# Matmuls on neighbouring strips of the TensorE array, queued as one group behind the member whose input comes last

## Chip, core and metric

The kernel runs on one core of one Trainium2 chip. The metric is device time in microseconds (us), the median of three timed runs. Besides these there is one profiled execution, whose records are what the views of the profile show.

## What is computed

Two layers of a diffusion backbone over 512 latent and 256 context tokens of width 1024, in float32. Layer 0 mixes tokens with neighbourhood attention (8 heads of 64) beside a chunked mLSTM; layer 1 with latent attention. Each layer then has a gated feed-forward part with hidden width 2816. In front of and behind each part stands an RMS norm:

```python
def rms_norm(x, g):
    xf = x.astype(jnp.float32)
    y = xf * lax.rsqrt(jnp.mean(xf * xf, axis=-1, keepdims=True) + EPS)
    return (y * g.astype(jnp.float32)).astype(x.dtype)
```

The change touches two things: the sums of squares under these norms, and in `neighbourhood_attention` the two products of the weights with the values, over the window and over the context keys:

```python
        return (jnp.einsum('bhqk,bkhd->bqhd', p[..., :nl], v_band)
                + jnp.einsum('bhqk,bkhd->bqhd', p[..., nl:], v_c))
```

## The kernel before

Activations lie feature-major: eight tiles of 128 features (index k or m) by 512 latent (`SX`, or its halves `SH`) and 256 context columns (`SC`). Each large product takes weights and activations split into a high and a low part, three matmuls for each piece of 128 features: `mm` (L139) is the helper that issues nearly all of them, so they all carry L139 and are told apart by their output tile: `yps` (output projections), `pu`/`puf` (feed-forward up), `pd`/`pdl` (feed-forward down; `pdl` is the last group), `qps`/`kvp` (the first projections of layer 1), `qp`/`sp` (queries and scores of the neighbourhood attention).

**Sums of squares.** A norm needs, for each token, a sum over 1024 features. The engines square the eight feature tiles one after another; `sums4` (L387) takes four squares at a time and issues four matmuls (L390) against a 128x32 matrix of ones. Each goes to its own strip of 32 columns of the array, and so to its own 32 partitions of one PSUM tile: `ysum` for the norm behind a part (`YNorm.put`, squares `ysq` made by ScalarE), `pss` for the norm ahead of the next part (`YNorm.chain` and `RawNorm.chain`, squares written over `acc`). Two calls make one sum. Then a chain runs over several engines (`sums_bc`, L393): ScalarE copies the sums (`srow`), TensorE adds the four strips (`psc`), VectorE and GpSimd form the inverse root (`rv`, `ry`), and TensorE spreads it over all partitions (`bcy` or `bcm`). `sums4` is called 30 times.

**Neighbourhood attention.** `na_attn` handles two heads at once. Head 0 uses array columns and output partitions 0 to 63, head 1 the other 64. For each block of 128 keys the transposed weights `pT` come from ScalarE for head 0 and from VectorE for head 1, and `products` (L879) issues matmuls into `ops`, the two heads in turn; L948 does the same for the context queries into `opc` from `ptc` (shown as `pTc`).

**What sets the order.** Each engine runs its instructions in one fixed order, made at build time by a scheduler of the framework from the program, the dependencies and its own estimate of when each input will be there. Matmuls of one call may therefore end up apart, with matmuls of other tiles between them.

Of the kernel before, what the change touches and what calls it, by code (L numbers as in the profile page):

```python
# [18 lines left out]
TX = 512  # L19
TC = 256  # L20
# [44 lines left out]
def hybrid_backbone_kernel(ctx: ExitStack, tc: tile.TileContext, *aps):  # L65
    nc = tc.nc
    V, S, G, PE = nc.vector, nc.scalar, nc.gpsimd, nc.tensor
    a = dict(zip(_DEV, aps))
    out = aps[len(_DEV)]
# [34 lines left out]
    def ps_x(name):  # L104
        return ps_t("x", name)
# [29 lines left out]
    V.memset(mhalf, -0.5)  # L135


    def mm(o, l, r, start, stop):
        PE.matmul(out=o, lhsT=l, rhs=r, start=start, stop=stop)  # L139

    def tr(o, i):
        PE.transpose(out=o, in_=i, identity=ident[0:i.shape[0], 0:i.shape[0]])  # L142
# [1 line left out]
    def act(o, i, func=AF.Copy, **kw):  # L144
        S.activation(out=o, in_=i, func=func, **kw)  # L145
# [35 lines left out]
    def proj(o, w, x, cols, ks=tuple(range(KD)), first=True, last=True):  # L181

        whi, wlo = w
        xhi, xlo = x
        for lo, hi, oo in cols:
            for k in ks:
                wh = whi[:, k * 128:(k + 1) * 128]
                wl = wlo[:, k * 128:(k + 1) * 128]
                oa = o[:, oo:oo + hi - lo]
                mm(oa, wh, xhi[:, k, lo:hi], first and k == ks[0], False)  # L190
                mm(oa, wh, xlo[:, k, lo:hi], False, False)
                mm(oa, wl, xhi[:, k, lo:hi], False, last and k == ks[-1])
# [38 lines left out]
    ones32 = const.tile([128, 32], F32, name="ones32")  # L231
# [154 lines left out]

    def sums4(ps, w, srcs, first, last):  # L387

        for i, src in enumerate(srcs):
            PE.matmul(out=ps[32 * i:32 * i + 32, 0:w], lhsT=ones32, rhs=src, start=first, stop=last,  # L390
                      tile_position=(0, 32 * i))

    def sums_bc(ps, sg, name):  # L393

# [7 lines left out]
    class YNorm:  # L402
# [10 lines left out]
        def put(self, m, src):  # L413
            w = self.sg.w
            if self.wide:
                if m == 0:
                    act(self.acc, src, AF.Square)
                else:
                    sq = scratch("ysq")
                    act(sq[:, :w], src, AF.Square)  # L420
                    tt(G, self.acc, self.acc, sq[:, :w], ALU.add)
                return
            if m % 2 == 0:
                self.t = sqp.tile([128, 512], F32, tag="sq", name="ysq")
            sq = self.t[:, 256 * (m % 2):256 * (m % 2) + w]
            act(sq, src, AF.Square)
            self.sq.append(sq)
            if m % 4 == 3:
                sums4(self.ps, w, self.sq[-4:], m == 3, m == KD - 1)

        def chain(self, x, y, Gt, mod=None, done=None):
# [13 lines left out]
            for k in range(KD):  # L445
                stt(y(k), y(k), Gt[:, k, c:c + 1], bc[:, :w], ALU.mult, ALU.mult)
                tt(G if k in (RVF if done and mod else RVO) else V, x(k), y(k), x(k), ALU.add)
                if mod:
                    act(y(k), x(k), AF.Square)
                    if k % 4 == 3:  # L450
                        sums4(ps2, w, [y(k - 3 + i) for i in range(4)], k == 3, k == KD - 1)
                else:
                    done(k)
                yield
# [17 lines left out]
    class RawNorm(YNorm):  # L472


        def chain(self, x, y, Gt, mod, done):
            sg = self.sg
            w, c = sg.w, sg.mc
            A, h = mod
            bc = sums_bc(self.ps, sg, "y")
            yield  # L480
            self.ps2 = ps_c("pss")
            for k in range(KD):
                stt(y(k), y(k), Gt[:, k, c:c + 1], bc[:, :w], ALU.mult, ALU.mult)
                tt(G if k in RVF else V, x(k), y(k), x(k), ALU.add)
                hi, lo = (t[:, k, sg.ho:sg.ho + w] for t in h)
                act(hi, x(k), AF.Copy, scale=A[:, k, c:c + 1])
                stt(lo, x(k), A[:, k, c:c + 1], fr(hi), ALU.mult, ALU.subtract)
                act(y(k), x(k), AF.Square)
                if k % 4 == 3:
                    sums4(self.ps2, w, [y(k - 3 + i) for i in range(4)], k == 3, k == KD - 1)  # L490
                yield
# [12 lines left out]
    with ExitStack() as l0:  # L504
# [20 lines left out]
        for k in range(KD):  # L525
            sq = x0p.tile([128, T], F32, tag="sq0", name="sq0", bufs=4)
            act(sq, x0[:, k, :], AF.Square)
            for lo, hi in ((0, TX), (TX, T)):
                PE.matmul(out=pss[32 * (k % 4):32 * (k % 4) + 32, lo:hi], lhsT=ones32, rhs=sq[:, lo:hi], start=k < 4,
                          stop=k >= 4, tile_position=(0, 32 * (k % 4)))  # L530
# [73 lines left out]
        for k in range(KD):  # L604
            for gp, lo, hi in ((gpx, 0, TX), (gpy, TX, T)):
                PE.matmul(out=gp[32 * (k % 4):32 * (k % 4) + 32, 0:hi - lo], lhsT=wg[:, k, :], rhs=x0[:, k, lo:hi],
                          start=k < 4, stop=k >= 4, tile_position=(0, 32 * (k % 4)))
# [87 lines left out]
        for i in range(7):  # L695
            src, dst = runs[i % 2], runs[1 - i % 2]
            for d in range(2):
                r = slice(32 * d, 32 * d + 32)
                o = 64 + (2 * d - 1) * 2 ** i
# [127 lines left out]
        def na_attn(p_, nw, bias_t, fill, qs, kd, kl, vtok):  # L827
            ops_ = ps_x("ops")
            nf = NF if p_ < 3 else NF3
            rows = ((0, 64), (64, 128))  # L830
# [32 lines left out]
            def turned(ks, Ps):  # L863

                pts = []
                for s, P in enumerate(Ps):
                    pt = ps_w("ptp")
                    for j in range(4):
                        tr(pt[:, j * 128:(j + 1) * 128], P[j][:, ks * 128:(ks + 1) * 128])
                    fill(nf[1])  # L870
                    pT = nw.tile([128, 512], F32, tag="pT", name="pT", bufs=4)
                    if s:
                        V.tensor_copy(out=pT, in_=pt)
                    else:
                        act(pT, pt)
                    pts.append(pT)
                return pts

            def products(ks, pts):  # L879

                if ks >= 2:
                    for s, (r0, r1) in enumerate(rows):
                        mm(ops_[r0:r1, 0:TX], vtok[:, 7 + ks - 2, r0:r1], pts[s], ks == 2, False)
                    return
                for j in range(4):
                    vi = VTILE[KSTART[j] + 16 * ks]
                    for s, (r0, r1) in enumerate(rows):
                        mm(ops_[r0:r1, j * 128:(j + 1) * 128], vtok[:, vi, r0:r1],
                           pts[s][:, j * 128:(j + 1) * 128], False, ks == 1 and j == 3)

            def scores_c(s):
                r0, r1 = rows[s]
# [20 lines left out]
            def turned_c(s, Pc):  # L913
                pt = ps_w("ptc")
                for kt in range(2):
                    for j in range(2):
                        tr(pt[:, (2 * kt + j) * 128:(2 * kt + j + 1) * 128],
                           Pc[:, j * 256 + kt * 128:j * 256 + (kt + 1) * 128])
                fill(nf[3])
                pT = nw.tile([128, 512], F32, tag="pT", name="pTc", bufs=4)  # L920
                if s:
                    V.tensor_copy(out=pT, in_=pt)
                else:
                    act(pT, pt)
                return pT
# [9 lines left out]
            for ks in (2, 3, 0, 1):  # L935
                pts = turned(ks, (P0, P1))
                if late:
                    products(*late)
                late = (ks, pts)
                if ks == 3:  # L940
                    cs.append(scores_c(1))
            ptc = [turned_c(0, cs[0])]
            products(*late)
            act(mix[:, p_, 0:TX].rearrange("p (r j c) -> p j r c", j=4, r=8),
                ops_.rearrange("p (j r c) -> p j r c", j=4, r=8))
            ptc.append(turned_c(1, cs[1]))
            opc = ps_x("opc")
            for kt in range(2):  # L948
                for s, (r0, r1) in enumerate(rows):
                    mm(opc[r0:r1, 0:TC], vtok[:, 7 + kt, r0:r1], ptc[s][:, kt * 256:(kt + 1) * 256],  # L950
                       kt == 0, kt == 1)
            act(mix[:, p_, TX:T], opc[:, 0:TC])


# [148 lines left out]
        with ExitStack() as nas:  # L1103
# [23 lines left out]
            for p_ in range(4):  # L1127
                cur, na0 = na0, []
                if p_ < 3:
                    nxt = na_proj(p_ + 1, nqr if p_ % 2 else nql, na0)  # L1130
                else:
                    for k in (4, 5, 6, 7, 0, 1, 2):
                        mix_split(k)
                    wo_first = [wload(a["w_out"][m]) for m in range(2)]
                    yp_first = ps_a("yps")
                    nxt = wo_steps()

                def fill(n):
                    for _ in range(n):
                        next(nxt, None)  # L1140

                na_attn(p_, nw, bias_t, fill, *cur)
                run(nxt)
# [636 lines left out]
```

## Time and profile before

| | |
|---|---|
| median of three runs | 1832.33 us (1832.32 to 1834.01) |
| the profiled execution | 1829.64 us |
| its span, first to last instruction | 1827.5 us |
| VectorE busy | 1162.9 us (64%) |
| ScalarE busy | 748.5 us (41%) |
| GpSimd busy | 254.6 us (14%) |
| DMA, mean | 89 GB/s |

The profile names TensorE's matmuls PE, its weight loads PEld, VectorE DVE, ScalarE ACT and GpSimd POOL. A float32 matmul leaves two records in it, one for each of two passes: "x2" is one matmul, "x8" four. A row of a timeline joins records that overlap or follow each other, and its second column is the time from the start of the first to the modelled end of the last. Since ends overlap, what a matmul costs the engine is read from the distance between starts.

### The profile page before, as it was taken

How to read it: one execution, taken by the hardware profiler on the slowest of the kernel's cores; microseconds unless marked ns; L12 is line 12 of the kernel's file. 1: busy time of each engine (PE TensorE's matmuls, PEld its weight loads, DVE VectorE, ACT ScalarE, POOL GpSimd, SP SyncE). 2: the span in 40 equal slices, each digit the busy share in tenths (PEclk: the TensorE clock that was granted, in tenths of full speed). 3: DMA queues.
4: the chain of work that ended last, by engine and by line, in shares of the span. 5: the costliest groups of instructions: out<-in, count | busy, mean ns of one | idle time of the engine just before them, and what ended most of it. 6: DMA issues, size and time to landing. Idle time of an engine off the chain costs nothing.

```text
span 1827.5 us, 26602 instructions
## 1 busy us (share of the span) xinstructions
PE 1768.6 (97%) x10498; PEld 1460.9 (80%) x10498; DVE 1162.9 (64%) x2210; ACT 748.5 (41%) x1297; POOL 254.6 (14%) x306
## 2 busy tenths in 40 slices
PE   6999999999999999999999999899999999999997
PEld 4777787887778888888888877788878888888885
DVE  3383677557356686776764655788894574556565
ACT  3333444444444422232221334577775354333241
POOL 1000123234320000000000001344441200000000
PEclk8999999999999999999999999999999999999998
DMA  9343322214212343434421211000012132224231
GB/s 308 110 127 127 123 86 81 62 55 133 76 35 93 125 131 114 134 120 135 131 83 47 91 36 47 24 12 13 13 35 84 47 104 90 95 81 136 72 93 47
DMA packets 63261, 162.39 MB, mean 89 GB/s; under 512 B 6273, under 2 KB 19793, under 8 KB 63137
## 3 DMA queue, kind: packets, MB, share of 16 engines
q1 hardware_dynamic: 61616, 156.52, 27.0%
q0 software_dynamic: 1376, 4.04, 0.7%
q8 instruction: 83, 1.36, 0.3%
q14 instruction: 42, 0.34, 0.1%
q10 hardware_dynamic: 144, 0.13, 0.0%
HBM read 158.57 MB, written 2.10 MB: 88 GB/s over the span
## 4 chain that ended last, share of the span: by engine, by line
PE 84%; DVE 6%; POOL 2%; issue 2%; ACT 2%; DMA 1%; DVEq 0%; POOLq 0%; ACTq 0%
PE pu L139 29%; PE pd L139 13%; PE yps L139 4%; PE sp L139 4%; PE qkp L139 3%; PE puf L139 3%; PE pdl L139 3%; PE vtk L139 3%; PE qp L139 2%; PE pt L142 2%; PE ot L139 2%; PE vp L139 2%; PE kp L139 2%; PE ops L139 1%; PE ysum L390 1%
## 5 line engine op out<-in xcount | busy, mean ns | idle before, releaser
L145 ACT ACTIVATE whi<-wraw 128x1024 fp32r<-128x1024 f32 x186 | 195.2, 1058 | 484.8 <-PE pu L139 219.8
L148 DVE TENSOR_TENSOR wlo<-wraw,whi 128x1024 fp32r<-128x1024 f32 x184 | 224.7, 1226 | 236.4 <-ACT whi L145 235.8
L139 PE MATMUL pu<-h,whi 128*128 128x258 f32 (+1 forms) x1280 | 318.5, 339 | 0.0
L139 PEld LDWEIGHTS pu<-h,whi 128*128 128x128 f32 x1280 | 219.6, 188 | 28.7 <-issue 0.8
L139 PE MATMUL pd<-hid,whi 128*128 128x512 f32 (+1 forms) x864 | 233.4, 358 | 1.2 <-DVE acc L148 1.2
L139 PE MATMUL pu<-h,wlo 128*128 128x512 f32 (+1 forms) x640 | 216.6, 339 | 0.0
L139 PEld LDWEIGHTS pd<-hid,whi 128*128 128x128 f32 x864 | 152.2, 188 | 28.2 <-DVE acc L148 2.8
L148 POOL TENSOR_TENSOR ry<-rv,mhalf 128x2 f32<-128x2 f32 (+2 forms) x26 | 23.0, 884 | 1017.9 <-DVE rv L151 1017.9
L139 PE MATMUL pd<-hid,wlo 128*128 128x512 f32 (+1 forms) x432 | 153.1, 356 | 0.0
L148 DVE TENSOR_TENSOR acc<-pd,acc 128x512 f32<-128x512 f32 (+1 forms) x192 | 109.0, 585 | 47.9 <-PE pd L139 46.6
L139 PEld LDWEIGHTS pu<-h,wlo 128*128 128x128 f32 x640 | 120.9, 189 | 13.6
L139 PE MATMUL pu<-hb,whi 128*128 128x512 f32 x304 | 119.8, 394 | 0.0
L139 PE MATMUL pu<-hb,wlo 128*128 128x512 f32 x304 | 119.2, 392 | 0.0
L139 PE MATMUL pu<-lb,whi 128*128 128x512 f32 x304 | 118.0, 388 | 0.0
L154 DVE SCALAR_TENSOR_TENSOR av<-aw,s,av 128x512 f32<-128x512 f32 x140 | 102.5, 748 | 23.2 <-DMA aw<-in_ada_w_dram 22.6
L151 POOL TENSOR_SCALAR P<-P,rl 128x768 f32<-128x768 f32 (+1 forms) x96 | 85.3, 890 | 143.1 <-DVE nm L151 49.8
L139 PEld LDWEIGHTS pd<-hid,wlo 128*128 128x128 f32 x432 | 81.2, 188 | 11.9
L154 DVE SCALAR_TENSOR_TENSOR u<-pu,c_ffn_conv,u 128x769 f32<-128x769 f32 x80 | 81.1, 1014 | 10.1 <-ACT u L145 9.4
L139 PE MATMUL sp<-kr,qh 128*128 128x512 f32 (+1 forms) x256 | 71.0, 353 | 2.5 <-ACT P L145 1.3
L148 DVE TENSOR_TENSOR pTl<-pt,pTh 128x512 fp32r<-128x512 f32 x96 | 64.5, 682 | 5.7 <-ACT pTh L145 4.9
L139 PEld LDWEIGHTS pu<-hb,wlo 128*128 128x128 f32 x304 | 57.1, 188 | 13.4
L139 PEld LDWEIGHTS pu<-lb,whi 128*128 128x128 f32 x304 | 57.1, 188 | 12.7
(454 smaller groups left out, 3840.1 us busy)
## 6 DMA issues: line engine op xcount, KB each, us to landing
wraw<-in_ffn_up_dram SPq DMA_DIRECT2D x88, 512.0 KB, 3.6
aw<-in_ada_w_dram SPq DMA_DIRECT2D x112, 256.0 KB, 2.7
wraw<-in_ffn_down_dram SPq DMA_DIRECT2D x44, 512.0 KB, 3.6
aw<-in_ada_w_dram SPq DMA_DIRECT2D x40, 512.0 KB, 4.5
wraw<-in_w_in_dram SPq DMA_DIRECT2D x20, 512.0 KB, 3.7
wraw<-in_w_tok_dram SPq DMA_DIRECT2D x8, 512.0 KB, 4.2
wraw<-in_w_out_dram SPq DMA_DIRECT2D x8, 512.0 KB, 3.7
wraw<-in_w_o_dram SPq DMA_DIRECT2D x8, 512.0 KB, 3.5
```

Source lines behind the costliest of these rows:

```text
L139: PE.matmul(out=o, lhsT=l, rhs=r, start=start, stop=stop)
L142: PE.transpose(out=o, in_=i, identity=ident[0:i.shape[0], 0:i.shape[0]])
L145: S.activation(out=o, in_=i, func=func, **kw)
L148: e.tensor_tensor(out=o, in0=x, in1=y, op=op)
L151: e.tensor_scalar(out=o, in0=x, scalar1=s1, scalar2=s2, op0=op0, op1=op1)
L154: V.scalar_tensor_tensor(out=o, in0=x, scalar=s, in1=y, op0=op0, op1=op1)
L390: PE.matmul(out=ps[32 * i:32 * i + 32, 0:w], lhsT=ones32, rhs=src, start=first, stop=last, tile_position=(0, 32 * i))
```

## The change

Three places get a group. In each, one matmul is issued first, the one that reads the input that the program makes last: in `sums4` the fourth square, in `products` and for `opc` the block of head 1. The other matmuls of the group are written inside `with tc.issue_after(...)`, which tells the scheduler that each of them must stand behind that first one in TensorE's order. It adds no wait on a semaphore, and the same matmuls write the same partitions.

```diff
     def mm(o, l, r, start, stop):
-        PE.matmul(out=o, lhsT=l, rhs=r, start=start, stop=stop)
+        return PE.matmul(out=o, lhsT=l, rhs=r, start=start, stop=stop)
...
     def sums4(ps, w, srcs, first, last):
 
-        for i, src in enumerate(srcs):
-            PE.matmul(out=ps[32 * i:32 * i + 32, 0:w], lhsT=ones32, rhs=src, start=first, stop=last,
-                      tile_position=(0, 32 * i))
+        def one(i):
+            return PE.matmul(out=ps[32 * i:32 * i + 32, 0:w], lhsT=ones32, rhs=srcs[i], start=first, stop=last,
+                             tile_position=(0, 32 * i))
+        n_ = len(srcs) - 1
+        with tc.issue_after(instr(one(n_))):
+            for i in range(n_):
+                one(i)
...
             def products(ks, pts):
 
-                if ks >= 2:
-                    for s, (r0, r1) in enumerate(rows):
-                        mm(ops_[r0:r1, 0:TX], vtok[:, 7 + ks - 2, r0:r1], pts[s], ks == 2, False)
-                    return
-                for j in range(4):
+                def one(s, j=0):
+                    r0, r1 = rows[s]
+                    if ks >= 2:
+                        return mm(ops_[r0:r1, 0:TX], vtok[:, 7 + ks - 2, r0:r1], pts[s], ks == 2, False)
                     vi = VTILE[KSTART[j] + 16 * ks]
-                    for s, (r0, r1) in enumerate(rows):
-                        mm(ops_[r0:r1, j * 128:(j + 1) * 128], vtok[:, vi, r0:r1],
-                           pts[s][:, j * 128:(j + 1) * 128], False, ks == 1 and j == 3)
+                    return mm(ops_[r0:r1, j * 128:(j + 1) * 128], vtok[:, vi, r0:r1],
+                              pts[s][:, j * 128:(j + 1) * 128], False, ks == 1 and j == 3)
+
+                with tc.issue_after(instr(one(1))):
+                    one(0)
+                    for j in range(1, 4 if ks < 2 else 1):
+                        one(1, j)
+                        one(0, j)
...
-            for kt in range(2):
-                for s, (r0, r1) in enumerate(rows):
-                    mm(opc[r0:r1, 0:TC], vtok[:, 7 + kt, r0:r1], ptc[s][:, kt * 256:(kt + 1) * 256],
-                       kt == 0, kt == 1)
+
+            def one_c(s, kt):
+                r0, r1 = rows[s]
+                return mm(opc[r0:r1, 0:TC], vtok[:, 7 + kt, r0:r1], ptc[s][:, kt * 256:(kt + 1) * 256],
+                          kt == 0, kt == 1)
+
+            with tc.issue_after(instr(one_c(1, 0))):
+                one_c(0, 0)
+                one_c(1, 1)
+                one_c(0, 1)
```

Every engine has the same instructions as before; only their order differs, nearly all of it on TensorE. Three places show it. A row below is one instruction of TensorE's order, or several equal ones (x2): source line, output tile, its two inputs, output size; the numbers tell buffers of one name apart. Since the change adds lines, L139 of before is L142 of the change, and L390 is L393.

First, the context product `opc` of the first pair of heads. Before (`pTc_3164` is head 0, `pTc_3180` head 1):

```order
L139 MATMUL sp_3198<-kl0_3034,qs0_2924 128x256
L139 MATMUL opc_3182<-pTc_3164,vtok_2527 64x256
L139 MATMUL sp_3198<-kd0_3032,qs0_2924 128x256
L139 MATMUL sp_3198<-kl0_3034,qs0_2924 128x256
L139 MATMUL opc_3182<-pTc_3180,vtok_2527 64x256
L139 MATMUL opc_3182<-pTc_3164,vtok_2527 64x256
L139 MATMUL opc_3182<-pTc_3180,vtok_2527 64x256
L139 MATMUL qp_3226<-h0_115,whi_3210 128x512
```

The same place of the change:

```order
L142 MATMUL sp_3198<-kd0_3032,qs0_2924 128x256
L142 MATMUL sp_3198<-kl0_3034,qs0_2924 128x256
L142 MATMUL qp_3226<-h0_115,whi_3210 128x512
L142 MATMUL qp_3226<-h1_116,whi_3210 128x512
L142 MATMUL opc_3182<-pTc_3180,vtok_2527 64x256
L142 MATMUL opc_3182<-pTc_3164,vtok_2527 64x256
L142 MATMUL opc_3182<-pTc_3180,vtok_2527 64x256
L142 MATMUL opc_3182<-pTc_3164,vtok_2527 64x256
L142 MATMUL qp_3226<-h0_115,wlo_3211 128x512
```

One matmul and a group of three have become one group of four, two `qp` matmuls later.

Second, the end of layer 0's feed-forward part, where the last down-projection of one half of the latent tokens (`pdl`, `ysum`) runs beside the norm of the other half (`pss`). Before:

```order
L390 MATMUL ysum_9716<-ysq_9731,ones32_93 32x256
L390 MATMUL pss_9749<-acc0_4394,ones32_93 32x256 x2
L390 MATMUL ysum_9716<-ysq_9731,ones32_93 32x256
L139 MATMUL pdl_9839<-hid0_9081,whi_9561 128x256
L139 MATMUL pdl_9839<-hid1_9082,whi_9561 128x256
L390 MATMUL ysum_9716<-ysq_9794,ones32_93 32x256
L139 MATMUL pdl_9839<-hid0_9081,wlo_9562 128x256
```

The change. The first group stands at the end of `pdl_9839`; the eight sums of these rows were spread over five stretches before, from the start of `pdl_9810` to the middle of `pdl_9881`:

```order
L142 MATMUL pdl_9839<-hid0_9489,wlo_9580 128x256
L393 MATMUL pss_9749<-acc0_4394,ones32_93 32x256 x4
L142 MATMUL pdl_9881<-hid0_9081,whi_9561 128x256
L142 MATMUL pdl_9881<-hid1_9082,whi_9561 128x256
L142 MATMUL pdl_9881<-hid0_9081,wlo_9562 128x256
L142 MATMUL pdl_9881<-hid0_9205,whi_9567 128x256
L142 MATMUL pdl_9881<-hid1_9206,whi_9567 128x256
L393 MATMUL ysum_9716<-ysq_9794,ones32_93 32x256
L393 MATMUL ysum_9716<-ysq_9731,ones32_93 32x256 x2
L393 MATMUL ysum_9716<-ysq_9794,ones32_93 32x256
L142 MATMUL pdl_9881<-hid0_9205,wlo_9568 128x256
```

Third, layer 1's first feed-forward projections (`puf`) beside the norm of the second half. Before, two of the places where squares were summed:

```order
L390 MATMUL pss_13845<-acc1_13270,ones32_93 32x256
L139 MATMUL puf_13892<-hb_12846,wlo_13783 128x256
L139 MATMUL puf_13892<-hb_12846,whi_13782 128x256
L139 MATMUL puf_13892<-lb4_12998,whi_13782 128x256
L390 MATMUL pss_13845<-acc1_13270,ones32_93 32x256
```

The change, at its first sum there:

```order
L142 MATMUL puf_13892<-hb_12846,whi_13776 128x256
L393 MATMUL pss_13845<-acc1_13270,ones32_93 32x256 x3
L142 MATMUL puf_13892<-lb4_12998,whi_13776 128x256
L142 MATMUL puf_13892<-hb_12846,wlo_13777 128x256
L142 MATMUL puf_13892<-hb_12846,whi_13776 128x256
L142 MATMUL puf_13892<-lb5_13139,whi_13776 128x256
L142 MATMUL puf_13892<-hb_12846,wlo_13777 128x256
L142 MATMUL puf_13892<-hb6_13142,whi_13776 128x256
L393 MATMUL pss_13845<-acc1_13270,ones32_93 32x256
```

Here the group of four is split into three and one, since the order only asks that the others stand behind the first, not right behind it; the second group of this norm stands whole, 26 `puf` matmuls later. Counting stretches of the order in which `sums4` matmuls stand together, there were 66 before and are 32 now: 28 whole groups of four, and two groups in two pieces.

More of the change, by code (lines that the diff above doesn't have):

```diff
@@ L135, in hybrid_backbone_kernel, with instr @@
     V.memset(mhalf, -0.5)
+    def instr(i):
+        return getattr(i, "ins", i)
     def mm(o, l, r, start, stop):
-        PE.matmul(out=o, lhsT=l, rhs=r, start=start, stop=stop)
+        return PE.matmul(out=o, lhsT=l, rhs=r, start=start, stop=stop)
     def tr(o, i):
```

## The prediction

> **What bounds the kernel now.** I read the page first, then TensorE's waits, then its timeline where the change acts.
>
> ```profile
> span 1827.5 us, 26602 instructions
> PE 1768.6 (97%) x10498; PEld 1460.9 (80%) x10498; DVE 1162.9 (64%) x2210; ACT 748.5 (41%) x1297; POOL 254.6 (14%) x306
> PE 84%; DVE 6%; POOL 2%; issue 2%; ACT 2%; DMA 1%; DVEq 0%; POOLq 0%; ACTq 0%
> ```
>
> TensorE is busy for 97% of the span and holds 84% of the chain that ended last. Time taken out of its stream therefore comes off the end, except where TensorE would then wait for another engine. Three rows of its waits from 490 us to 1820 (total, times, longest):
>
> ```profile
> PE bcy L142 <- DVE ry L154: 5.2, 8, 1.7
> PE ysum L390 <- ACT ysq L145: 1.7, 3, 0.8
> PE pss L390 <- ACT acc L145: 1.4, 3, 0.5
> ```
>
> TensorE waits at `bcy` for the norm chain, and at the sums for squares that come late. These are the places where a gain can be lost again.
>
> **What a stretch of sums costs.** By a stretch I mean `sums4` matmuls with no other matmul between them. TensorE's timeline (start, length, engine, line, output<-inputs, shapes, count; a length reaches to the modelled end, so I take distances between starts):
>
> ```profile
> 502.47 0.40 PE L139 MATMUL yps<-h,whi 128*128 128x256 f32 x2
> 502.70 0.28 PE L139 MATMUL yps<-h,wlo 128*128 128x256 f32 x1
> 502.91 0.63 PE L390 MATMUL ysum<-ysq,ones 128*32 128x256 f32 x6
> 503.47 0.51 PE L139 MATMUL yps<-h,whi 128*128 128x256 f32 x2
> 503.81 0.28 PE L139 MATMUL yps<-h,wlo 128*128 128x256 f32 x1
> 504.03 0.62 PE L390 MATMUL ysum<-ysq,ones 128*32 128x256 f32 x2
> 504.58 0.50 PE L139 MATMUL yps<-h,whi 128*128 128x256 f32 x2
> 504.92 0.28 PE L139 MATMUL yps<-h,wlo 128*128 128x256 f32 x1
> ```
>
> An ordinary matmul takes 0.12 here (two in 0.23, from 502.47 to 502.70). From 503.81 to 504.92 pass 1.11 us, in which three of them start, worth 0.35. The one sum between them costs the other 0.76: 0.10 ahead of it, 0.55 of its own, 0.11 behind it. From 502.70 to 503.81 it is 1.11 again, with three sums in the stretch. And four:
>
> ```profile
> 533.86 0.64 PE L390 MATMUL pss<-acc,ones 128*32 128x256 f32 x8
> ```
>
> Four last 0.64 where one lasts 0.62. So **a stretch costs about 0.75 us whether it holds one sum or four**. [...] Sums of 512 columns cost more:
>
> ```profile
> 500.66 1.04 PE L390 MATMUL pss<-acc,ones 128*32 128x512 f32 x2
> 501.64 0.51 PE L139 MATMUL yps<-h,whi 128*128 128x256 f32 x2
> ```
>
> Here 0.98 stands in place of 0.55, so 1.18 in all.
>
> **The sums, stage by stage.** The busy time of L390 alone in six windows (window, its length, PE busy, records, PEld busy, clock, DMA share, GB/s):
>
> ```profile
> 490.00:545.00 55.00, 7.99 (x48) 1.46 (x48) 1.00 0.12 39
> 1060.00:1102.00 42.00, 9.76 (x48) 2.33 (x48) 1.00 0.08 26
> 1102.00:1129.00 27.00, 6.65 (x32) 1.63 (x32) 1.00 0.18 53
> 1129.00:1150.00 21.00, 4.95 (x16) 1.10 (x16) 1.00 0.18 57
> 1385.00:1455.00 70.00, 10.31 (x64) 2.43 (x64) 1.00 0.26 84
> 1785.00:1827.50 42.50, 5.04 (x32) 1.19 (x32) 0.89 0.15 50
> ```
>
> The fourth window holds eight sums, each alone: 8 x 0.62 = 4.96. Counted in the timeline the windows hold 10, 15, 10, 8, 16 and 7 stretches, together 66. Ten at 0.62 explain 6.2 of the third; 0.43 more is a stretch in which two `ysum` want the same strip, and the second follows the first. The second window has one such too, the fifth a smaller one (0.3). The order of the change has 6, 7, 4, 2, 9 and 4 stretches, together 32, and none that mixes two tiles. So **34 stretches go**: two of 512 columns (2.4), 32 at 0.75 (24.0), and 1.2 for the mixed ones; some 30 groups that grow to four cost 0.4 together. That is **27.2 us** for TensorE by itself.
>
> **The attention's products.** First `opc`, with one head-0 product alone and then three:
>
> ```profile
> 378.78 0.65 PE L139 MATMUL opc<-pTc,vtok 128*64 128x256 f32 x2
> 379.36 0.38 PE L139 MATMUL sp<-kd,qs 128*128 128x256 f32 x1
> ...
> 379.79 1.08 PE L139 MATMUL opc<-pTc,vtok 128*64 128x256 f32 x6
> 380.80 0.73 PE L139 MATMUL qp<-h,whi 128*128 128x512 f32 x2
> ```
>
> Alone it takes 0.58, with the borders of above 0.78. The three take 1.01, which is two rounds (0.58 and 0.43), since two of them belong to head 1; four are two rounds as well. So 0.78 goes in each of four pairs of heads: 3.1. In `ops`, two products of 512 columns of the last pair come together that stood apart; by the row at 500.66 one costs 1.18, I take 1.1, because the neighbours there are short transposes. In the other three pairs one that stood alone joins the next stretch, whose rest of five becomes four: one round less.
>
> ```profile
> 330.50 1.10 PE L139 MATMUL ops<-pT,vtok 128*64 128x128 f32 x16
> 331.53 0.65 PE L142 MATMUL ptc<-c_ident,Pc 128*128 128x128 f32 x4
> ...
> 333.39 0.44 PE L139 MATMUL ops<-pT,vtok 128*64 128x128 f32 x4
> 333.76 0.44 PE L142 MATMUL vtp<-c_ident,vt 128*128 128x128 f32 x2
> ```
>
> One round of two takes 0.37 to the next start, four rounds 1.03, so a further one 0.22; three times that is 0.6. Together **4.8 us**. TensorE shows no wait for these inputs, so I take all of it.
>
> **What comes back as waits.** Between a `bcy` and the next squares VectorE, ScalarE and GpSimd work at their own pace, and TensorE now gets there sooner. The three places with most of it, TensorE and ScalarE by turns:
>
> ```profile
> 1439.12 0.40 PE L142 MATMUL bcy<-c_ident,ry 128*128 128x128 f32 x2 [0.53 <-DVE ry L154]
> ...
> 1444.44 0.62 PE L390 MATMUL pss<-acc,ones 128*32 128x256 f32 x4 [0.39 <-ACT acc L145]
> ```
>
> ```profile
> 1443.66 1.34 ACT L145 ACTIVATE acc<-x 128x256 f32<-128x256 f32 x4 [1.84 <-POOL x L148]
> ```
>
> After 1439.12 the change has 26 `puf` matmuls (3.1) and the broadcast (0.4) ahead of the group whose head reads the fourth square, so TensorE is there at 1442.6. ScalarE makes that square from 1443.66 on, held up by GpSimd; a quarter of its row later, at 1444.0, it is ready. A wait of 1.4 takes the place of the 0.4 at 1444.44, and this group is one of those in two pieces: about **1.1** comes back.
>
> ```profile
> 1081.53 0.43 PE L142 MATMUL bcy<-c_ident,ry 128*128 128x128 f32 x2 [0.21 <-DVE ry L154]
> ```
>
> ```profile
> 1087.39 0.40 ACT L145 ACTIVATE acc<-x 128x256 f32<-128x256 f32 x1
> ```
>
> After 1081.53 stand 37 `pdl` matmuls (4.4), so TensorE could be there at 1086.3, but the fourth square is the one of 1087.39, ready at 1087.8: 1.5 lost, and 0.2 at the `ysum` group behind it, against waits of about 1.0 at single sums that go: **0.7**. The next half (from 1104) is built alike, but two broadcasts behind it that waited are now reached later in the order: nothing net.
>
> ```profile
> 522.68 0.62 PE L390 MATMUL ysum<-ysq,ones 128*32 128x256 f32 x2 [0.78 <-ACT ysq L145]
> ```
>
> This sum waits for a square that doesn't move; two `puf` more stand ahead of it in the change, so 0.4 of its 0.75 is gained: **0.3** back. Some six `bcy` and `bcs` have one or a few matmuls fewer ahead of them: 0.1 each, **0.6**. The kernel's last chain starts at its last square and ends as before. Together 2.7.
>
> 27.2 + 4.8 - 2.7 = **29.3 us**. The profiled execution took 1829.64, 2.1 more than its span and 2.7 less than the median of the three runs; what goes is all inside the span. 1829.64 becomes 1800.3, and the median of 1832.33 becomes **1803**.
>
> **The rivals.**
>
> *The waits eat more.* I worked out the new arrival at few places. If the loss of 1.1 of layer 1's feed-forward stage came at eleven more of the 32 heads, 12 us would come back: saving 17, **1815**. Against it: only 3.1 us of TensorE's present waits are for squares, in six places.
>
> *Nothing comes back.* Saving 32 and some 2 of the present waits: **1798**. It needs the squares to be earlier by as much as TensorE is.
>
> *Slower: the heads block the queue.* A group now begins with its last input, and what stands behind a waiting matmul waits with it, `pdl` and `puf` included. 32 us gross over 32 groups is 1.0 each: a longer mean wait at the heads makes the kernel slower; at 1.5 it is 48 - 32 = 16 more, **1848**. [...] But the longest wait for a square now is 0.8, and all of them together are 3.1.
>
> *It doesn't do what it says.* If a group that begins with its last strip didn't run side by side, each would cost 0.75 + 3 x 0.43 = 2.0, 32 of them 65 where 66 cost 51 before: 14 more, and 1842 with the products' 4.8 still gained. Against it stands 333.39: this stretch begins with head 1, and its two products take 0.37 together.
>
> **How the numbers follow.** My forecast has a chance of 0.72, with 1798 to 1809 as its own range (5 us of waits that I didn't see, either way); more waits 0.15; nothing back 0.08; the two slower ones 0.03 and 0.02. The range 1797 to 1815 takes in the first three and their bounds. About 0.2% (3.7 us) is what a measurement can tell from no change. Faster by more 0.94, within it 0.02, slower 0.04.
>
> **What would show it.** Right: the sums' busy time near 21 us in place of 44.7 over the six windows, nearly all as rows x8 of 0.64; `opc` only x8; TensorE's busy time down by some 30, and its longest new wait at the first `pss` behind `bcy` in layer 1's first feed-forward stage. Wrong: rows x8 that last over 1 us at 256 columns (strips in series), waits of over 1 us for `ysq` or `acc` at many groups, or a wait at `bcy` and `bcm` that grows behind each shortened stretch.

## The result, and the profile after

| | before | with the change |
|---|---|---|
| median of four runs each | 1832.32 us (1830.69 to 1834.01) | 1806.62 us (1805.91 to 1807.70) |
| ratio of the two | | 0.9858 (95% interval 0.9845 to 0.9870) |
| span of the profiled execution | 1827.5 us | 1804.3 us |

The change saves 25.7 us. The prediction was 29.3 us (1803.0, with a range from 1797 to 1815). The question for the experiments is where the other four went.

The page of the changed kernel, the lines that answer to those of before (L393 of the change is L390 of before, L142 is L139, L145 the transposes' L142):

```profile
span 1804.3 us, 26608 instructions
PE 1739.2 (96%) x10498; PEld 1454.0 (81%) x10498; DVE 1163.0 (64%) x2210; ACT 748.2 (41%) x1297; POOL 253.7 (14%) x306
PE 83%; DVE 7%; POOL 3%; issue 2%; DMA 2%; ACT 2%; DVEq 0%; POOLq 0%; ACTq 0%
```

TensorE's matmuls leave the same 10498 records, and it is busy for 29.4 us less (1768.6 before); no other engine's busy time moves by more than 0.9. It is still the bound. Now the busy time of the sums alone, in six windows that hold the same work as those of the prediction (window, its length, PE busy, records, PEld busy, clock, DMA share, GB/s):

```profile
487.00:539.00 52.00, 4.69 (x48) 0.94 (x48) 1.00 0.12 41
1054.00:1094.00 40.00, 4.45 (x48) 1.07 (x48) 0.96 0.08 27
1094.00:1114.00 20.00, 2.56 (x32) 0.63 (x32) 1.00 0.26 80
1114.00:1133.00 19.00, 1.28 (x16) 0.32 (x16) 1.00 0.18 56
1367.00:1434.00 67.00, 6.01 (x64) 1.52 (x64) 1.00 0.29 87
1762.00:1804.00 42.00, 2.56 (x32) 0.63 (x32) 0.88 0.16 51
sum 240.00, PE 21.54 PEld 5.11; mean PE 3.59 PEld 0.85
```

44.7 us have become 21.5. The fourth window says it most plainly: the same 16 records took 4.95 as eight stretches and take 1.28 as two. TensorE's waits from 490 us to 1800 (total, times, longest), the rows that stood ahead of the prediction:

```profile
PE bcy L145 <- DVE ry L157: 4.4, 7, 1.7
PE pss L393 <- ACT acc L148: 3.8, 5, 1.2
PE ysum L393 <- ACT ysq L148: 2.8, 3, 1.1
```

The waits for squares have grown from 3.1 us to 6.6. They did not become many: eight groups wait where six single sums did.

**Stage by stage.** I take the starts of the same seven matmuls in both traces and the distances between them, in us (in the change they start at 304.48, 488.75, 538.03, 1054.74, 1143.87, 1453.66 and 1795.21). The first column says where each stretch of the program begins and ends; the forecast is the prediction's sum, put to the stages by its stretches and waits.

| from ... to | before | change | saved | forecast |
|---|---|---|---|---|
| `hTp` (302.46) to the first `bcy` (491.17): attention's products | 188.71 | 184.26 | 4.5 | 4.8 |
| to a `bcm` (544.00): output projection, front of feed-forward | 52.83 | 49.29 | 3.5 | 3.6 |
| to a `pd` (1060.68): feed-forward, layer 0 | 516.68 | 516.71 | 0.0 | 0 |
| to a `bcs` (1162.14): end of layer 0, start of layer 1 | 101.47 | 89.13 | **12.3** | **15.2** |
| to the first `pu` of layer 1 (1475.27) | 313.13 | 309.79 | 3.3 | 4.4 |
| to the last `bcy` (1818.41) | 343.14 | 341.55 | 1.6 | 2.3 |
| small terms (broadcasts 0.6, grown groups 0.4) | | | | -1.0 |
| sum | | | 25.2 | 29.3 |

25.2 us of the 29.3 are there. (The span shows only 23.2 of them, because `hTp` itself starts 2.0 us later in this execution; nothing of the change stands ahead of it. More on that below.) Of what is missing, 2.9 us are missing in one stage, the end of layer 0, 1.1 in layer 1 and 0.7 in the last stage.

### The profile page after: what moved, and what is told of

Its sections match the earlier page's. It is cut to its first block, busy times and chain, and to the rows that moved or that the text cites. A ratio compares the mean times of both kernels' runs of the same rounds, so it can differ in the third digit from the quotient of the medians.

```text
span 1804.3 us, 26608 instructions
## 1 busy us (share of the span) xinstructions
PE 1739.2 (96%) x10498; PEld 1454.0 (81%) x10498; DVE 1163.0 (64%) x2210; ACT 748.2 (41%) x1297; POOL 253.7 (14%) x306
## 3 DMA queue, kind: packets, MB, share of 16 engines
q1 hardware_dynamic: 61616, 156.52, 27.6%
## 4 chain that ended last, share of the span: by engine, by line
PE 83%; DVE 7%; POOL 3%; issue 2%; DMA 2%; ACT 2%; DVEq 0%; POOLq 0%; ACTq 0%
PE pu L142 29%; PE pd L142 14%; PE sp L142 4%; PE qkp L142 3%; PE yps L142 3%; PE puf L142 3%; PE vtk L142 3%; PE pdl L142 3%; PE qp L142 2%; PE ot L142 2%; PE pt L145 2%; PE vp L142 2%; PE kp L142 2%; DMA aw<-in_ada_w_dram 1%; DVE acc L157 1%
## 5 line engine op out<-in xcount | busy, mean ns | idle before, releaser
L142 PE MATMUL pu<-h,whi 128*128 128x258 f32 (+1 forms) x1280 | 318.5, 339 | 0.0
L142 PEld LDWEIGHTS pu<-h,whi 128*128 128x128 f32 x1280 | 219.6, 188 | 28.7 <-issue 0.8
L142 PE MATMUL pd<-hid,whi 128*128 128x512 f32 (+1 forms) x864 | 233.4, 358 | 1.5 <-DVE acc L151 1.5
L142 PE MATMUL pu<-h,wlo 128*128 128x512 f32 (+1 forms) x640 | 216.6, 339 | 0.0
L142 PEld LDWEIGHTS pd<-hid,whi 128*128 128x128 f32 x864 | 152.2, 188 | 28.6 <-DVE acc L151 3.1
L142 PE MATMUL pd<-hid,wlo 128*128 128x512 f32 (+1 forms) x432 | 153.1, 356 | 0.0
L142 PEld LDWEIGHTS pu<-h,wlo 128*128 128x128 f32 x640 | 120.9, 189 | 13.7
L142 PE MATMUL pu<-hb,whi 128*128 128x512 f32 x304 | 119.5, 393 | 0.0
L142 PE MATMUL pu<-hb,wlo 128*128 128x512 f32 x304 | 119.3, 392 | 0.0
L142 PE MATMUL pu<-lb,whi 128*128 128x512 f32 x304 | 118.2, 389 | 0.0
L142 PEld LDWEIGHTS pd<-hid,wlo 128*128 128x128 f32 x432 | 81.2, 188 | 11.9
L142 PE MATMUL sp<-kr,qh 128*128 128x512 f32 (+1 forms) x256 | 71.0, 353 | 2.5 <-ACT P L148 1.3
L142 PEld LDWEIGHTS pu<-hb,wlo 128*128 128x128 f32 x304 | 57.1, 188 | 13.1
L142 PEld LDWEIGHTS pu<-lb,whi 128*128 128x128 f32 x304 | 57.1, 188 | 12.8
```

Of the source, the lines that this page charges most:

```text
L142: return PE.matmul(out=o, lhsT=l, rhs=r, start=start, stop=stop)
```

## Experiments

All ratios are to the kernel before, run in the same batch. My theory: a stretch costs 0.75 us however many sums it holds, so the saving counts stretches; what is missing is waited at the heads of the groups, for squares that are made late.

**1. The two parts apart.** `sums_only` has the group in `sums4` and the old attention; `products_only` the reverse, whose edit to the change is

```diff
-        n_ = len(srcs) - 1
-        with tc.issue_after(instr(one(n_))):
-            for i in range(n_):
-                one(i)
+        for i, src in enumerate(srcs):
+            PE.matmul(out=ps[32 * i:32 * i + 32, 0:w], lhsT=ones32, rhs=src, start=first, stop=last,
+                      tile_position=(0, 32 * i))
```

> The group in sums4 alone; the attention's products as before. Theory (a stretch of narrow matmuls costs its 0.75 us however few it holds, and the two parts of the change add up): 32 stretches of sums as in the change, and the products' 4.8 us are not gained, so 1806.6 + 4.8 = 1811.4 us, ratio to before 0.9886. Rival (part of the 4.8 is lost elsewhere anyway, since the trace of the change has a new wait of 1.1 us inside the attention): 1808, ratio 0.987. Rival (the parts hinder each other, and the sums alone gain the 24.5 us forecast for them): 1807.8.

Measured: 1811.29 us, ratio 0.9881 (0.9868 to 0.9895).

> The attention's products and opc grouped, sums4 as before, with its 66 stretches. Theory: 4.8 us below before, 1827.5 us, ratio 0.9974, and in the profile opc in rows x8 only. Rival (the wait of 1.1 us of the change's trace eats into it): 1829 to 1830, ratio 0.999.

Measured: 1827.67 us, ratio 0.9977 (0.9968 to 0.9986); `opc` comes in one piece:

```profile
338.36 1.08 PE L142 MATMUL opc<-pTc,vtok 128*64 128x256 f32 x8
```

Against the batch's 1832.42 the parts save 21.1 and 4.8 us by the medians, together 25.9, and the change saves 25.7: they add up. By the intervals of the ratios the sums save 19.2 to 24.2 and the products 2.6 to 5.9. So the products' 4.8 meets its forecast within about 1.7 us, and the error is in the sums, 21.1 where 24.5 (27.2 less 2.7) was expected.

**2. Is it the number of stretches?** `later10` traces the groups at a lower priority, so that 16 more stretches arise:

```diff
+        with tc.high_priority(offset=-10):
+          sums4_(ps, w, srcs, one)
+
+    def sums4_(ps, w, srcs, one):
         n_ = len(srcs) - 1
         with tc.issue_after(instr(one(n_))):
```

> The change, with the groups of sums4 traced at a lower priority (offset -10), so that other matmuls get between the members of some groups: 48 stretches of sums in place of 32, all 16 more of them of 256 columns. Theory (0.75 us a stretch): the sums' share grows by 16 x 0.75 = 12 us, and at most 3 us of the waits at the groups' heads go: 1815.6 to 1818.6. Rival (what the change gains is that the groups stand late in the order, not that they stay together): 1806 or less.

Measured: 1819.86 us (1818.80 to 1822.20), ratio 0.9930 (0.9917 to 0.9944): 13.2 above the change, 1.3 over the upper end of the theory and nowhere near the rival. At 0.75 each the 16 stretches make 12.0 of it. What I had wrong is that waits would go and nothing come for them; in this profile they are (from 490 us on)

```profile
PE pss L393 <- ACT acc L148: 3.4, 5, 1.2
PE pdl L142 <- DVE acc L151: 3.1, 5, 1.0
```

With 1.7 at `ysum` the heads wait 5.1 us in place of 6.6, and `pdl` (1.7 in the change) waits 1.4 longer. A group that has been broken up still begins with its last square.

**3. Fewer stretches still.** `eight` makes one group of the eight sums of each `pss` tile:

```diff
+        if first:
+            held.append((ps, srcs))
+            return
+        n = next(i for i, h_ in enumerate(held) if h_[0] is ps)
+        a, b = held.pop(n)[1], srcs
...
+        with tc.issue_after(instr(one(3, b[3], True))):
+            for i in range(3):
+                one(i, b[i], True)
+            for i in (3, 0, 1, 2):
+                one(i, a[i], False)
```

> The change, with the eight sums of a pss tile issued as one group behind the eighth square, in place of two groups of four: 23 stretches of sums in place of 32, seven of them of two rounds or more. Theory (a stretch costs by itself, a second round on the same strips 0.43): 9 x 0.75 = 6.8 us go, 8 x 0.43 = 3.4 come back, and the second round stands behind the last square on the chain of each norm, which costs up to 0.43 at the five or so norms whose broadcast TensorE waits for (2 us): 1803 to 1806. Rival (the norm's chain is what counts: the heads now wait for the eighth square at every pss group, and the broadcasts come later by more): 1809 or more.

Measured: 1804.82 us, ratio 0.9847 (0.9834 to 0.9861): within the theory's range. The groups' rows, the first of 512 columns and the second of 256:

```profile
502.69 1.92 PE L414 MATMUL pss<-acc,ones 128*32 128x512 f32 x16
535.20 1.07 PE L414 MATMUL pss<-acc,ones 128*32 128x256 f32 x16
```

Eight sums of 256 columns last 1.07 where four last 0.64: a second round on the same strips costs 0.43, less than a second stretch.

**4. The change once more.** Between 1056.9 and 1060.3 us the profile of the change shows something that before does not. Three rows of TensorE's timeline in the change (start, length, count):

```profile
1056.68 0.59 PE L142 MATMUL pdl<-hid,whi 128*128 128x256 f32 x2 [0.62 <-DVE acc L151]
...
1057.29 1.06 PE L142 MATMUL pdl<-hid,whi 128*128 128x256 f32 x4
1058.15 0.41 PE L142 MATMUL pdl<-hid,wlo 128*128 128x256 f32 x1
```

Four matmuls start between 1057.29 and 1058.15, 0.21 apart, where such matmuls take 0.12 elsewhere (products of the split parts leave one record each, so that x4 is four of them; the sums and `opc` leave two: 240 matmul and 240 weight-load records for 120 sums). The clock granted to TensorE there is 0.51. To see whether the change brings this about, it ran again unaltered (`change_again`).

> The change itself, unaltered, for a second profile and more times. Theory (the half-clock stretch of 3.4 us at 1057 us of its first profile is the luck of where a clock window falls against a wait that before has too): the same waits of 0.9 and 0.6 us at the pd and pdl matmuls near 1055 us, but the half-clock stretches elsewhere or not at all; median 1806 to 1807. Rival (the change itself brings it about): again half clock from about 1057 us, for 3.4 us.

Measured: 1808.53 us (1806.06 to 1809.00), ratio 0.9863 (0.9846 to 0.9879). The median is 1.5 us above the expected range, while the ratio is that of the first time; the profiled execution is the fastest of the four. Two windows of the change (PE, PEld, DVE, ACT and POOL busy, clock, DMA share, GB/s):

```profile
1053.50:1056.90 3.40, 1.88 (x10) 1.34 (x10) 3.35 (x6) 1.77 (x2) 0.00 (x0) 1.00 0.00 0
1056.90:1060.30 3.40, 3.40 (x18) 3.40 (x18) 3.09 (x5) 0.88 (x2) 0.00 (x0) 0.51 0.28 66
```

and of the second profile, the same two and one more:

```profile
1053.50:1056.90 3.40, 2.27 (x11) 1.40 (x9) 3.35 (x6) 1.15 (x2) 0.00 (x0) 1.00 0.00 0
1056.90:1060.30 3.40, 2.85 (x21) 2.65 (x22) 3.28 (x5) 1.50 (x2) 0.00 (x0) 1.00 0.16 13
...
507.30:510.70 3.40, 3.40 (x18) 3.40 (x17) 2.73 (x4) 1.54 (x4) 0.76 (x1) 0.50 0.02 5
```

The half-clock stretch has moved to 507.3 us (0.50) and the one at 1057 is gone (1.00), with the same waits ahead of it (0.90 and 0.61 us at 1055.35 and 1057.29, in the first profile 0.90 and 0.62). The stage from `pd` to `bcs` takes 88.24 us here, 0.89 less than in the first profile. So 0.9 of the 2.9 us missing in that stage is the luck of that execution, and the rival falls.

**5. Do the heads wait because squares are late?** `sq_first` makes each square ahead of the split `h` of the same tile, in `RawNorm` alone:

```diff
+                act(y(k), x(k), AF.Square)
                 act(hi, x(k), AF.Copy, scale=A[:, k, c:c + 1])
                 stt(lo, x(k), A[:, k, c:c + 1], fr(hi), ALU.mult, ALU.subtract)
-                act(y(k), x(k), AF.Square)
```

> The change, with RawNorm making each square ahead of the split h of the same tile, so that the squares under pss come one ScalarE instruction (0.41 us) earlier in layer 0's feed-forward part. Theory (the expected gain that is missing went into waits of the groups' heads for late squares): TensorE's waits at pss for acc near 1080, 1098 and 1120 us fall from 0.6 to 0.9 each to 0.2 to 0.5 each, 1.2 us in all: 1805.4. Rival (the heads wait for something else that comes last, or h is then late for the projections): the waits move to qps or stay, 1806.6 or more.

Measured: 1806.82 us, ratio 0.9856 (0.9839 to 0.9873). The times can't tell it from the change, so I read the stage. TensorE's waits from 1062 us to 1150 in the unaltered change (`change_again`):

```profile
PE pss L393 <- ACT acc L148: 2.3, 3, 0.9
PE bcy L145 <- DVE ry L157: 1.1, 3, 0.4
PE pdl L142 <- DVE acc L151: 0.8, 2, 0.6
```

and in `sq_first`:

```profile
PE bcy L145 <- DVE ry L157: 1.7, 3, 0.7
PE pdl L142 <- DVE acc L151: 1.1, 2, 0.6
PE pss L393 <- ACT acc L148: 1.0, 3, 0.4
```

The heads' waits fall by 1.3, as the theory says of them. But `bcy` and `pdl` take 0.9 of it back, and the stage from `pd` to `bcs` takes 88.88 us against 88.24: the gain isn't there. **In this stage most of the wait moves on; it doesn't go.** What is left of it is outweighed by something else: in this stage TensorE is busy for 83.5 us against 82.4, though the sums take 8.3 in both. The same ordinary matmuls cost more in the new order, and why is not shown. My theory was right about the cause of the waits and wrong about what they are worth here.

**6. The same for layer 1.** There GpSimd's additions hold the squares up. `adds_dve` puts all of them on VectorE; `chain_adds` only those in `YNorm.chain` (layer 1, and behind layer 0's output projection):

```diff
-                tt(G if k in (RVF if done and mod else RVO) else V, x(k), y(k), x(k), ALU.add)
+                tt(V if mod else G if k in RVO else V, x(k), y(k), x(k), ALU.add)
```

> The change, with all additions x + y of the norms on VectorE (0.41 us each) in place of five in eight there and three in eight (two in eight) on GpSimd (0.73 to 1.64), so that the late squares come earlier. Theory (heads wait for squares that GpSimd holds up; a stretch costs 0.75 us): the waits of the heads at 1121 (0.88) and 1423 us (1.19) and 0.41 at 1397 go down to under 1.0 together, 1.5 gained; the order has 27 stretches of sums in place of 32, three of them of two rounds, 5 x 0.75 - 3 x 0.43 = 2.4 more: 1802 to 1804. Rival (VectorE, which makes the norm's product ahead of each square, gets so much more that all squares come later): longer waits at pss and ysum, 1807 to 1810.

Measured: 1804.25 us, ratio 0.9839 (0.9824 to 0.9853), just above the theory's range.

> The change, with the additions x + y on VectorE only in YNorm.chain (layer 0 behind its output projection, layer 1 ahead of its feed-forward part), and on GpSimd as before in RawNorm (the end of layer 0's feed-forward part). Theory (an earlier square is worth its wait where TensorE has nothing else to wait for, in layer 1's stage; in layer 0's last stage the wait only moves on to the broadcasts): all of what the kernel with the additions everywhere gained comes from 1395 to 1440 us, 3.2 us, so some 1804, and the stage from 1052 to 1160 us takes as long as in the change. Rival (the gain needs both stages): 1806 or more.

Measured: 1804.24 us, ratio 0.9846 (0.9833 to 0.9860). Both intervals meet that of the change (0.9845 to 0.9870), so what they gain has to be read from the stages. The two times are the same, so the additions at the end of layer 0 give nothing that the times show, though they are what brought the order of `adds_dve` from 30 stretches, as in `chain_adds`, down to 27. (The clock at that place is not shown for `adds_dve`, so its stage isn't set beside the others.) In `chain_adds` the stage from `pd` to `bcs` takes 88.24 us, as in the change without half clock, and the one from there to `pu` 307.8 us against 309.8 and 309.9 in the change's two profiles: 2.0 to 2.2 of the expected 3.2 us. TensorE's waits in layer 1, from 1360 us to 1437, in the change:

```profile
PE pss L393 <- ACT acc L148: 1.6, 2, 1.2
PE bcy L145 <- DVE ry L157: 1.4, 2, 0.7
PE bcm L145 <- DVE ry L157: 1.3, 2, 0.7
PE ysum L393 <- ACT ysq L148: 0.8, 1, 0.8
```

and in `chain_adds`:

```profile
PE bcy L145 <- DVE ry L157: 1.4, 2, 0.7
PE bcm L145 <- DVE ry L157: 1.3, 2, 0.7
PE ysum L393 <- ACT ysq L148: 1.2, 1, 1.2
```

Here the wait at `pss` goes, the one at `ysum` is 0.4 longer, and the broadcasts wait no longer than they did: 1.2 us less of waiting, about half of the gain. The other half comes from the order. From 1393 us to `pu` TensorE's timeline has five stretches of sums in place of seven, and the sums are busy there for 3.6 us in place of 4.7. So an earlier square seems to be worth its wait in this stage, but the run does not part the two: `eight`, which makes no square earlier, takes 307.8 us for this stage as well.

**7. Put together.** `eight_adds` is `eight` with `adds_dve`; `mixed` is `chain_adds` with the groups of eight in `YNorm.chain` alone, so that the end of layer 0 stays as in the change.

> The groups of eight and the additions on VectorE together: 23 stretches of sums, 16 of four and seven of eight. Theory (the gains are of different kinds and add up; of the 2.4 us by fewer stretches in the kernel with the additions alone nothing is left, since the stretches are as many as with the groups of eight alone): 1804.8 less the shorter waits at the heads, 1.0 to 1.5, so 1803.3 to 1803.8. Rival (with the head at the eighth square the chain behind it decides, and an earlier square only moves the wait to the broadcast): 1804.8 or more.

Measured: 1805.48 us, ratio 0.9842 (0.9827 to 0.9857): no better than `eight` alone, as the rival had it.

> The same, and in YNorm.chain one group of eight sums in place of two of four: 27 stretches of sums. Theory (a stretch less gains 0.75, a second round costs 0.43, where TensorE is the bound): 1.0 to 1.5 us behind the output projection, near 500 to 540 us, and in layer 1 about as much as with the additions alone; 1802.5 to 1803.5. Rival (the head at the eighth square costs as much in later broadcasts as the four stretches less gain): 1804 or more.

Measured: 1801.49 us (1799.83 to 1803.12), ratio 0.9830 (0.9817 to 0.9843), 1.0 us below the theory's range: faster than before, and than the change by intervals that only just don't meet (0.9845 to 0.9870 in its own batch). Against `chain_adds` it saves 1.4 us from `bcy` to `bcm` (47.89 against 49.33), 0.6 up to `pd` (516.05 against 516.68), and 0.3 in layer 1 (307.5 from `bcs` to `pu`).

## Why the prediction came out as it did

**The price of a stretch: right.** 0.75 us was read from two rows a microsecond apart; the "borders" in the forecast for `opc` are its 0.10 ahead of a stretch and 0.11 behind it, and what fills them no run shows. `later10` (16 more, 13.2 us) and the sums' busy time (44.7 down to 21.5, forecast near 21) agree with it; `opc` comes only as x8, and TensorE's busy time is down by 29.4 ("some 30").

**The products: right.** 4.8 forecast, 4.8 in `products_only` by the medians, and 4.3 in its profile from `hTp` to the first `bcy` (184.37 us in place of 188.71). The change's profile has a new wait of 1.1 at `spc` for VectorE in the attention; in exchange the half-clock stretch that the profile of before has at 302.6 us (0.50 up to 306.0) is absent there (1.00).

**The largest new wait: right in place, and near in size.** "The first `pss` behind `bcy` in layer 1's first feed-forward stage", forecast as 1.4 with the group in two pieces:

```profile
1418.40 0.40 PE L145 MATMUL bcy<-c_ident,ry 128*128 128x128 f32 x2 [0.69 <-DVE ry L157]
...
1423.05 0.63 PE L393 MATMUL pss<-acc,ones 128*32 128x256 f32 x6 [1.19 <-ACT acc L148]
1424.52 0.62 PE L393 MATMUL pss<-acc,ones 128*32 128x256 f32 x2
```

Three sums wait 1.19 us, and the fourth stands apart behind six `puf`.

**The term "waits that come back", 2.7 us: too small.** This is the term that was mis-sized: I worked out the new arrival at five places, and waits arose at heads where I had put none. Over the whole stretch from the first `bcy` to the last, TensorE's idle time grew by 4.4 us (24.7 to 29.1, the gaps between modelled ends and starts in the trace), 1.7 more than forecast. (The second profile has 27.6. My estimate is that its half clock from 507.3 to 510.7 us, granted 0.50, fills about 1 us of a wait with slower work: TensorE's waits for `ysq` at `ysum` and `yps` together are 2.1 us there and 3.1 in the first profile.) Two heads that I didn't look at:

```profile
1121.00 0.64 PE L393 MATMUL pss<-acc,ones 128*32 128x256 f32 x8 [0.88 <-ACT acc L148]
```

Of this tile's eight squares before summed each alone, over 13 us, and waited for none; the head now stands ahead of the square. And

```profile
1397.00 0.93 PE L393 MATMUL pss<-acc,ones 128*32 128x256 f32 x8 [0.41 <-ACT acc L148]
```

which shows a second flaw of mine and of the change: this group lasts 0.93 and not 0.64, because one of its four, which waits for a square of its own, starts 0.3 us behind the head. ScalarE made that group's last squares from 1396.53 on, after a wait for GpSimd's `x`: the fourth square, which the program issues last, need not be the last to be made (so I read it), since GpSimd takes 0.85 for an addition and VectorE 0.41. I had booked the 0.3 of the mixed stretch in this stage as a gain; it stayed.

The place that I gave 0.7 to (the fourth square behind 1081.53) came out at 0.8, TensorE's idle time from that `bcy` to the next `bcm` going from 0.5 to 1.3, but otherwise than I said: the wait at the first `pss` went from 0.54 to 0.68 only, and a `pdl` behind the broadcast now waits 0.6 for VectorE.

The third head is the kernel's last group. There the wait grew from 0.40 to 0.97, since three of its sums used to run in that time. Before and in the change:

```profile
1813.96 0.63 PE L390 MATMUL ysum<-ysq,ones 128*32 128x256 f32 x6
1815.00 0.62 PE L390 MATMUL ysum<-ysq,ones 128*32 128x256 f32 x2 [0.40 <-ACT ysq L145]
```

```profile
1791.74 0.64 PE L393 MATMUL ysum<-ysq,ones 128*32 128x256 f32 x8 [0.97 <-ACT ysq L148]
1792.89 0.61 PE L142 MATMUL psc<-sel,srow 128*128 128x1 f32 x4 [0.51 <-ACT srow L148]
```

"The last chain starts at its last square and ends as before" holds, but then the stretch that ran ahead of that square can't be gained in full, and I had booked all three stretches of this stage: it saved 1.6 us of 2.3. The three heads' new waits, 0.88, 0.41 and 0.57, make 1.9, about what the term lacks.

**The bookkeeping.** Behind the attention the forecast was 24.5 (27.2 less 2.7), and the first profile shows 20.8. Of the 3.7 us between them, waits make 1.7 (4.4 against 2.7), the half clock at 1057 us 0.9, and the straggler at 1397.00 another 0.3. Some 0.8 I could not place. Most of it lies between `pd` and `bcs`: without waits TensorE's matmuls save 15.0 us there in the second profile, where 20 stretches, the mixed ones and the grown groups come to 15.6. `sq_first`, with 1.1 us more for the same matmuls, shows that a new order of them can cost as much, but that was not tried apart, and this stays open.

**The rivals.** "The waits eat more" (1815) named the mechanism, but of the 12 us that it put on top 1.7 came. "The heads block the queue" needs a mean wait of 1.0 at 32 heads; it is 6.6 / 32 = 0.2. That what stands behind a waiting matmul waits with it shows in both traces: TensorE was idle for 0.78 us ahead of 522.68 before, and for 0.88 ahead of 1121.00 in the change. Strips in series would have made rows x8 of over 1 us; they are 0.64.

## What to carry to other kernels

Count how often a narrow matmul stands alone between full ones: each such stretch cost TensorE 0.75 us here whether it held one or four, and two rounds in a stretch cost 0.43 more, so keep together what shares the array. The group at 1397.00 suggests putting a group behind the member that is made last in time, not last in the program; that was not tried. Look at each head in the stage's own waits: whether an earlier input pays depends on what waits behind it and on what the new order does to the rest, as layer 1 (2.0 to 2.2 us gained, half of it by fewer stretches) and the end of layer 0 (none) show. When two profiles differ by a microsecond, look at the granted clock ahead of the instructions.

## What the hardware showed unexpectedly

Half clock came and went in executions of one and the same kernel. In the change's first profile TensorE was granted half clock for 3.41 us from 1056.95 (0.51 over 1056.9 to 1060.3). In the 3.40 us from 1053.5 it had been idle for 1.52, in two waits of 0.90 and 0.62. `mixed` has half clock near there too (0.83 over 1052 to 1062, as in the change). In `change_again` the same two waits, 0.90 and 0.61, are followed by full clock (1.00 up to 1063.7); its half clock (0.50) runs from 507.3 to 510.7, behind 0.96 us of idle time from 503.9 on, where the first profile has 0.96 as well and then 1.00. In before, 2.10 us idle from 299.2 to 302.6 stand ahead of half clock (0.50 up to 306.0); in the change 1.88 idle from 302.6 to 306.0 and 1.59 from 1149.1 to 1152.5 were followed by 1.00. So the idle time of the 3.4 us ahead does not decide alone. In the profiles of before and of the change, each stretch between two changes of the granted clock, from 32.9 us on and up to the last change, lasted a whole number of 3.41 us: 1 or 2 at half clock, and 33, 45, 215, 265 or 443 at full clock. The theory for `change_again` has it that the place of a wait on such a grid decides; these figures don't settle that. A half-clock stretch cost 0.9 us near 1057 (89.13 in place of 88.24 from `pd` to `bcs`) and 0.4 near 507 (49.69 in place of 49.29 from `bcy` to `bcm`).

Half clock also makes some 1.2 of the 2.0 us by which `hTp` is late: from 142 us to 160 the granted clock is, in before and in the change,

```profile
142.00:160.00 18.00, 15.04 (x92) 12.20 (x92) 4.64 (x6) 6.07 (x14) 0.00 (x0) 0.91 0.40 136
```

```profile
142.00:160.00 18.00, 14.26 (x82) 11.63 (x82) 4.39 (x5) 4.74 (x13) 0.00 (x0) 0.81 0.38 137
```

The change's execution has half clock (0.50) there from 145.59 to 152.42 us and that of before from 145.54 to 148.95, ahead of anything that the change touches; the `sTp` that starts at 149.08 in before comes 0.89 us later in the change, the `qkp` at 150.44 comes 2.04 later. Another 0.9 us is a longer wait for a transfer of weights, again in before and in the change:

```profile
145.98 1.08 PE L252 MATMUL ada<-aw,s 128*32 128x256 f32 x8 [1.69 <-DMA aw<-in_ada_w_dram]
```

```profile
146.76 1.08 PE L255 MATMUL ada<-aw,s 128*32 128x256 f32 x8 [2.61 <-DMA aw<-in_ada_w_dram]
```

`hTp` starts at 302.20 in `sums_only` and at 304.34 in `products_only`, so its start moves by 2 us between executions whatever the change does behind it.
